# Layer two's mixers' output and MLP: the two parts of a chunk side by side in one strip of 512 columns

## The chip, the cores and the metric

The kernel runs on one core of a Trainium2 chip. The metric is the time of one execution on the device in microseconds (us). TensorE (PE) multiplies; VectorE (DVE), ScalarE (ACT) and GpSimd (POOL) do the elementwise work; SyncE (SP) issues the transfers from the chip's main memory.

## The reference

Two layers of a trunk on 16 learned meta tokens and 256 tokens, width 2048. The part around the change, cut:

```python
def _layer(h, w_in, ..., w_out, ln1_w, ln1_b, w_ff1, w_ff2, ln2_w, ln2_b):
    proj = jnp.einsum('bld,dp->blp', h, w_in)
    ...
    mix = jnp.einsum('blm,md->bld', jnp.concatenate([y_gla, y_na], axis=-1), w_out)
    h = _layer_norm(DEEPNORM_ALPHA * h + mix, ln1_w, ln1_b)
    ff = jnp.einsum('blf,fd->bld', jnp.square(jax.nn.relu(jnp.einsum('bld,df->blf', h, w_ff1))), w_ff2)
    return _layer_norm(DEEPNORM_ALPHA * h + ff, ln2_w, ln2_b)
```

The meta tokens are dropped at the end, so the second layer needs them only as keys and values: after its projection it works on T = 256 columns, where the first layer works on L = 272.

## The kernel before, in words

Activations lie transposed: a chunk is 128 features (partitions) by up to 272 tokens (columns), and 16 chunks make the width. Each is kept as two float32r parts, a high one (the rounded value) and a low one (what the rounding left), and so is each weight. A product is the sum of three: high weight by high part, high weight by low part, low weight by high part.

`three` (L156 to 167) issues them for one chunk and one tile of 128 weight columns. With 272 columns it is three matmuls, L165, L166, L167. With exactly 256 (`n == T`) the first two are one matmul of 512 columns over `x.joined` (L161), and the third (L162) adds the low weights' share onto the second half of the bank; what evicts the bank adds the halves. So in layer two each chunk and weight tile cost a **pair**, L161 and L162.

`by_m` runs over output tiles, and for each over all chunks with `three`, 16 pairs for a tile of the output (32 in the MLP's second product, which takes y and u). `by_k` (L191) runs over chunks first, with four output tiles open; it multiplies high and low part separately, also where there are 256 columns. It is used where chunks become ready one by one: the first 512 outputs of the mixers' output product, and the third group of the MLP's first product. The first two groups of that product run on chunks that aren't normalised yet and carry two columns more (`n + 2`, 258 in layer two), so they take the three matmuls.

`made` (L141 to 154) loads a weight tile of 128 x 1024 (512 KB), rounds it into `wh` on ScalarE (L152) and subtracts on VectorE for `wl` (L153); `weights` keeps two tiles ahead, the pools hold three. `order` yields the tiles in the order of use: 12 groups of the projection, 4 of the mixers' output, then the MLP. Nothing but this order and the code's own order sets what comes when around the change: a queue of generators (`fg`, `bg`) is stepped between the matmul groups, and SP issues the weights' transfers only.

Places: a chunk's two parts lie in one tile of 640 columns (`ROOM`), the first from column `home` on and the second `apart` columns later (`WIDE[layer]`); weights start at `STARTS[layer]` in a tile of 1088 columns. The tiles of x, y, u, wh and wl all begin at 64 modulo 256 bytes, so a start of 3 columns is byte 76 modulo 256. In layer two the parts are 288 columns apart, so that `x.joined` is two runs of 256 columns with a gap of 32 between them.

The chunks are x (the residual stream; written by `ln_add`, and again, normalised, by `renew`), y (the mixers' outputs, later half of the MLP's inner activations) and u (the other half). Layer two's x also serves its projection, where keys and values need all 272 columns.

Of the kernel before, what the change touches and what calls it, by code (L numbers as in the profile page):

```python
# [17 lines left out]
T = 256  # L18
# [18 lines left out]


ROOM = 640
WIDE = (23, 276), (3, 288)  # L40
STARTS = (40, 48), (0, 8)


class Pair(tuple):
# [7 lines left out]
class Trunk:  # L52
# [71 lines left out]
    def order(self):  # L124

        i, first = self.i, [4, 2]
        for l in range(DEPTH):
            groups = [i["win"][l, g] for g in range(12)] + [i["wout"][l, g] for g in range(4)]
            for half in range(2):
                groups += [i["wff1"][l, 8 * half + g] for g in range(8)] + [i["wff2"][l, half, g] for g in range(4)]  # L130
            for w in groups:
                for t in range(w.shape[0]):
                    yield w[t], first.pop(0) if first else 1, l

    def weights(self):

# [4 lines left out]
    def made(self, ap, parts, l):  # L141
        if ap is None:
            return None
        nc = self.nc
        size = ap.shape[-1]
        raw = self.wp.tile([P, WB], F32, name="raw", tag="raw")[:, :size]
        wh, wl = (self.wp.tile([P, WB + 64], F32R, name=nm, tag=nm)[:, at:at + size]
                  for nm, at in zip(("wh", "wl"), STARTS[l]))
        for p in range(parts):
            c = slice(p * size // parts, (p + 1) * size // parts)  # L150
            nc.sync.dma_start(raw[:, c], ap[:, c])
            nc.scalar.copy(wh[:, c], raw[:, c])  # L152
            self.wl = nc.vector.tensor_tensor(wl[:, c], raw[:, c], wh[:, c].bitcast(F32), ALU.subtract).ins  # L153
        return wh, wl
# [67 lines left out]
    def pair(self, pool, name, c, late=None):  # L222
        if name == "sp":
            return Pair(pool.tile([P, 2, L], F32R, name=f"{name}{c}", tag=f"{name}{c}", bufs=1))
        t = pool.tile([P, ROOM], F32R, name=f"{name}{c}", tag=f"{name}{c}", bufs=1)
        return self.parts(t, *WIDE[1 if (self.l if late is None else late) else 0])

    def parts(self, t, home, apart):

        both = t[:, home:home + 2 * apart].rearrange("p (a c) -> p a c", a=2)  # L230
        made = Pair(both)
        made.joined = both[:, :, :T]
        return made


# [214 lines left out]
    def gla_head(self, h):  # L450
# [48 lines left out]
        for at, lv in enumerate(order):  # L499
            q, k = ahead  # L500
            ahead = operands(order[at + 1]) if at + 1 < len(order) else across()
            ps = self.bank()
            for b in (slice(0, P), slice(P, T)):
                r = b if lv < 8 else slice(P - b.start, T - b.start)
                nc.tensor.matmul(ps[:, b], lhsT=k[:, b], rhs=q[:, r], start=True, stop=True)  # L505
            if full and lv <= 4:
                nc.tensor.matmul(ps[:, T:L], lhsT=k[:, T:T + P], rhs=q[:, T:L], start=True, stop=True)
            p2 = ps[:, :T].rearrange("p (s c) -> p s c", s=2)
            if lv >= 7:
                nc.scalar.copy(A[:, 0:5:4, :] if lv == 7 else A[:, 1:4:2, :], p2)  # L510
            else:
                nc.vector.copy_predicated(A[:, 0:5:4, :], self.mask[:, lv:lv + 1, :].to_broadcast([P, 2, P]), p2)
            if full and lv == 0:
                nc.vector.tensor_copy(Am[:, T:L], ps[:NM, T:L])
            elif full and lv <= 4:
                nc.vector.copy_predicated(Am[:, T:L], self.mask[:NM, lv, :NM], ps[:NM, T:L])
            yield
# [353 lines left out]
    def renew(self, end):  # L871

        f = self.norm
        n = f["n"]
        for c in range(f["new"], end):
            while f["ready"] <= c:
                self.step(self.bg, 1)
            h, lo = self.x[c]
            self.split(self.acc[:, c, :n], h[:, :n], lo[:, :n])
        f["new"] = end  # L880
# [138 lines left out]
```

## Time and profile before

| | us |
|---|---|
| median of 3 runs | 2386.49 |
| lowest, highest | 2386.22, 2386.54 |
| the profiled execution | 2386.44 |
| its span, first to last instruction | 2384.2 |

The stages of layer two, by the profile's timeline: projection and mixers from about 1237 to 1557 us, the mixers' output from 1557 to 1651, the MLP's first two groups on unnormalised chunks to 1698, the group by chunks to 1721, then the rest of the MLP to 2366, and the last normalisation.

How to read the rows: a group of instructions has its line, engine, operation, output and inputs by the program's names, the shape and the count, then busy time in us, mean duration in ns, and the idle time of the engine ahead of them with what ended it. A window has its ends, its length, each engine's busy time with the count of instructions that touch it, the granted clock, the share of the DMA engines and GB/s. A timeline row has a start, a duration (us), engine, line, operation and shape. A matmul's end is modelled, so that rows overlap: the pace is read from starts.

### The profile page before, as it was taken

What the parts mean: (1) busy time and instruction counts of PE and PEld (TensorE: products, weight loads), DVE (VectorE), ACT (ScalarE), POOL (GpSimd) and SP (SyncE); (2) the same over time, 40 slices, a digit from 0 to 9 for tenths busy, and PEclk for the clock granted to TensorE, in tenths of its full rate; (3) what the DMA queues carried; (4) which work ended last, traced back from release to release, by engine and by line L of the source; (5) the groups of instructions that cost most, each with busy time, mean ns of one, the idle gap of its engine ahead of it and who ended that gap; (6) DMA issues with size and microseconds to landing.
All of it is one profiled execution on the core that took longest, in us unless ns stands there. A gap on an engine that the chain in (4) does not pass through costs nothing.

```text
span 2384.2 us, 43078 instructions
## 1 busy us (share of the span) xinstructions
PE 2351.7 (99%) x17276; PEld 2230.9 (94%) x17276; DVE 1576.1 (66%) x2473; ACT 1187.5 (50%) x1962; POOL 283.5 (12%) x447
## 2 busy tenths in 40 slices
PE   9999999999999999999999999999999999999997
PEld 9999999999999999999999899999988888888886
DVE  6688787775544455557577887878766555666655
ACT  6555555564433344444456655555644333444443
POOL 1164320010000000000020554200100000000000
PEclk9999999999999999999999999999999999999998
DMA  7544445555555556555555445456656665656563
GB/s 248 168 142 146 143 140 160 178 179 183 178 182 180 178 181 182 178 181 179 180 177 183 142 148 153 149 160 189 192 189 191 189 190 189 190 190 191 189 188 131
DMA packets 118359, 417.46 MB, mean 175 GB/s; under 512 B 13388, under 2 KB 16332, under 8 KB 118160
## 3 DMA queue, kind: packets, MB, share of 16 engines
q1 hardware_dynamic: 118160, 414.72, 55.7%
q8 instruction: 135, 2.21, 0.4%
q14 instruction: 64, 0.52, 0.1%
HBM read 412.57 MB, written 2.10 MB: 174 GB/s over the span
## 4 chain that ended last, share of the span: by engine, by line
PE 92%; DVE 4%; POOL 2%; issue 1%; ACT 1%; DMA 0%; SPq 0%; ACTq 0%; POOLq 0%; DVEq 0%
PE mm L161 22%; PE mm L165 16%; PE mm L166 16%; PE mm L167 16%; PE mm L162 11%; PE mm L191 6%; POOL lev L475 1%; PE bg L505 1%; DVE wl L153 1%; PE bg L648 1%; DVE acc L864 1%; PE bg L597 1%; ACT wh L152 0%; ACT ns L580 0%; DVE lev L481 0%
## 5 line engine op out<-in xcount | busy, mean ns | idle before, releaser
L153 DVE TENSOR_TENSOR wl<-raw,wh 128x1024 fp32r<-128x1024 f32 (+1 forms) x772 | 945.9, 1226 | 628.7 <-ACT wh L152 620.4
L152 ACT CAST wh<-raw 128x1024 fp32r<-128x1024 f32 (+1 forms) x772 | 803.4, 1041 | 916.4 <-PE mm L166 334.0
L165 PE MATMUL mm<-x,wh 128*128 128x272 f32 (+2 forms) x2176 | 624.2, 287 | 0.0
L166 PE MATMUL mm<-x,wh 128*128 128x272 f32 (+2 forms) x2176 | 617.9, 284 | 0.0
L167 PE MATMUL mm<-x,wl 128*128 128x272 f32 (+2 forms) x2176 | 617.2, 284 | 0.1
L166 PEld LDWEIGHTS mm<-x,wh 128*128 128x128 f32 x2176 | 409.3, 188 | 0.0
L165 PEld LDWEIGHTS mm<-x,wh 128*128 128x128 f32 x2176 | 407.8, 187 | 1.2 <-issue 0.4
L167 PEld LDWEIGHTS mm<-x,wl 128*128 128x128 f32 x2176 | 407.8, 187 | 0.5 <-DVE wl L153 0.3
L161 PE MATMUL mm<-x,wh 128*128 128x512 f32 x1152 | 403.5, 393 | 0.0
L162 PE MATMUL mm<-x,wl 128*128 128x256 f32 x1152 | 320.2, 278 | 0.2 <-DVE wl L153 0.2
L161 PEld LDWEIGHTS mm<-x,wh 128*128 128x128 f32 x1152 | 215.7, 187 | 48.5 <-issue 0.4
L161 PE MATMUL mm<-y,wh 128*128 128x512 f32 x704 | 245.7, 391 | 0.0
L162 PEld LDWEIGHTS mm<-x,wl 128*128 128x128 f32 x1152 | 215.6, 187 | 0.7 <-DVE wl L153 0.6
L166 PE MATMUL mm<-y,wh 128*128 128x272 f32 x704 | 199.2, 283 | 0.0
L165 PE MATMUL mm<-y,wh 128*128 128x272 f32 x704 | 199.2, 283 | 0.0
L167 PE MATMUL mm<-y,wl 128*128 128x272 f32 x704 | 198.9, 283 | 0.0
L162 PE MATMUL mm<-y,wl 128*128 128x256 f32 x704 | 195.4, 278 | 0.6 <-DVE wl L153 0.6
L161 PE MATMUL mm<-u,wh 128*128 128x512 f32 x512 | 178.9, 391 | 0.0
L475 POOL TENSOR_TENSOR lev<-be 128x128 f32<-128x128 f32 (+1 forms) x256 | 150.2, 616 | 115.4 <-PE bg L505 36.4
L161 PEld LDWEIGHTS mm<-y,wh 128*128 128x128 f32 x704 | 132.1, 188 | 29.1
L165 PE MATMUL mm<-u,wh 128*128 128x272 f32 x512 | 144.9, 283 | 0.0
L166 PE MATMUL mm<-u,wh 128*128 128x272 f32 x512 | 144.9, 283 | 0.0
(235 smaller groups left out, 3314.0 us busy)
## 6 DMA issues: line engine op xcount, KB each, us to landing
raw<-in_wff SPq DMA_DIRECT2D x512, 512.0 KB, 3.5
raw<-in_win SPq DMA_DIRECT2D x190, 512.0 KB, 3.5
raw<-in_wout SPq DMA_DIRECT2D x64, 512.0 KB, 3.5
nb<-in_nab SPq DMA_DIRECT2D x16, 352.0 KB, 4.3
out<-acc SPq DMA_DIRECT2D x8, 256.0 KB, 2.2
xraw<-in_xT SPq DMA_DIRECT2D x7, 272.0 KB, 5.1
wraw<-in_wup SPq DMA_DIRECT2D x2, 392.0 KB
raw<-in_win SPq DMA_DIRECT2D x4, 128.0 KB, 3.1
```

The costliest lines, as they stand in the source:

```text
L152: nc.scalar.copy(wh[:, c], raw[:, c])
L153: self.wl = nc.vector.tensor_tensor(wl[:, c], raw[:, c], wh[:, c].bitcast(F32), ALU.subtract).ins
L161: mm(ps, lhsT=wh[:, c:c + P], rhs=x.joined, start=first, stop=False)
L162: mm(ps[:, T:], lhsT=wl[:, c:c + P], rhs=xh[:, :T], start=False, stop=last)
L165: mm(o, lhsT=wh[:, c:c + P], rhs=xh[:, :n], start=first, stop=False)
L166: mm(o, lhsT=wh[:, c:c + P], rhs=xl[:, :n], start=False, stop=False)
L167: mm(o, lhsT=wl[:, c:c + P], rhs=xh[:, :n], start=False, stop=last)
L191: self.nc.tensor.matmul(ps[m][:, :n], lhsT=parts[p][0][:, c:c + P], rhs=acts[j][parts[p][1]][:, :n], start=j + p == 0, stop=j == nk - 1 an ...
L475: tt = lambda o, x, y: nc.gpsimd.tensor_tensor(o, x, y, ALU.subtract)
L505: nc.tensor.matmul(ps[:, b], lhsT=k[:, b], rhs=q[:, r], start=True, stop=True)
L597: nc.tensor.matmul(ps[hh][:, t * NKEY:t * NKEY + NKEY], lhsT=q[hs, NM + t * P:NM + t * P + P], rhs=k[hs, t, :], start=True, stop=True)
L648: nc.tensor.matmul(r[hs], lhsT=(v2 if rest else v1)[:, t, hs], rhs=p2[:, t, :] if rest else p1[:, 2 * t + hh, :], start=rest, stop=not rest)
```

## The change

Layer two's y and u get a third place, (20, 256): the first part at column 20, the second right behind it at 276. `joined` is then one run of 512 columns. Layer two's x keeps its place through the projection and the first two groups of the MLP, and gets the new one when `renew` writes the normalised chunk, if there are 256 columns. The weights of layer two's mixers' output and MLP (`j > 11` of the groups) start at 36 and 4 columns in place of 0 and 8.

```diff
-WIDE = (23, 276), (3, 288)
-STARTS = (40, 48), (0, 8)
+WIDE = (23, 276), (3, 288), (20, T)
+STARTS = (40, 48), (0, 8), (36, 4)
...
-            for w in groups:
+            for j, w in enumerate(groups):
                 for t in range(w.shape[0]):
-                    yield w[t], first.pop(0) if first else 1, l
+                    yield w[t], first.pop(0) if first else 1, l + (l and j > 11)
...
-        return self.parts(t, *WIDE[1 if (self.l if late is None else late) else 0])
+        return self.parts(t, *WIDE[(2 if name != "x" else 1) if (self.l if late is None else late) else 0])
...
-        made.joined = both[:, :, :T]
+        made.tile, made.joined = t, t[:, home:home + 2 * T] if apart == T else both[:, :, :T]
...
             while f["ready"] <= c:
                 self.step(self.bg, 1)
+            if n == T:
+                self.x[c] = self.parts(self.x[c].tile, *WIDE[2])
             h, lo = self.x[c]
```

What the matmuls on float32r read in the two programs, in layer two (bytes modulo 256 of the start of the moving columns and of the weights; counts are of matmuls):

| matmuls | chunks before | weights before | chunks after | weights after |
|---|---|---|---|---|
| projection, x: 320 of 512 columns, 320 of 256, triples of 272 and 274, by chunks of 272 | 76, 204 | 64, 96 | the same | the same |
| pairs on x, y, u: 2048 of 512 columns | 76 and, 1152 bytes on, 204 | 64 | 144, one run | 208 |
| the same: 2048 of 256 columns | 76 | 96 | 144 | 80 |
| by chunks, x and y: 384 of 256 columns | 76, 204 | 64, 96 | 144, 144 | 208, 80 |
| 128 triples of 258 columns, x | 76, 204 | 64, 96 | 76, 204 | 208, 80 |

Layer one reads its chunks at 156 and 236 and its weights at 224 and 0 in both. On every engine the instructions stand in the same order, with the same waits, in both programs; only addresses and the shape of that one access differ.

## The prediction

> **What bounds the kernel now.** I read the page first: the busy shares, the row of the granted clock and the chain that ended last.
>
> ```profile
> span 2384.2 us, 43078 instructions
> PE 2351.7 (99%) x17276; PEld 2230.9 (94%) x17276; DVE 1576.1 (66%) x2473; ACT 1187.5 (50%) x1962; POOL 283.5 (12%) x447
> PEclk9999999999999999999999999999999999999998
> PE 92%; DVE 4%; POOL 2%; issue 1%; ACT 1%; DMA 0%; SPq 0%; ACTq 0%; POOLq 0%; DVEq 0%
> PE mm L161 22%; PE mm L165 16%; PE mm L166 16%; PE mm L167 16%; PE mm L162 11%; PE mm L191 6%; POOL lev L475 1%; PE bg L505 1%; DVE wl L153 1%; PE bg L648 1%; DVE acc L864 1%; PE bg L597 1%; ACT wh L152 0%; ACT ns L580 0%; DVE lev L481 0%
> ```
>
> TensorE sets the end: busy 99%, its clock at full all along, its lines 92% of the chain. But a busy matmul row says little about how fast matmuls follow each other, since their ends are modelled and overlap. What counts here is the distance from start to start. So I next took the groups of lines 161 and 162 from 1557 us (where layer two's mixers' output begins) to the end, and then windows and timelines inside stretches in which only one kind of matmul runs.
>
> ```profile
> L161 PE MATMUL mm<-x,wh 128*128 128x512 f32 x832 | 288.5, 391 | 0.0
> L161 PE MATMUL mm<-y,wh 128*128 128x512 f32 x704 | 245.7, 391 | 0.0
> L162 PE MATMUL mm<-x,wl 128*128 128x256 f32 x832 | 231.0, 278 | 0.0
> L162 PE MATMUL mm<-y,wl 128*128 128x256 f32 x704 | 195.4, 278 | 0.6 <-DVE wl L153 0.6
> L161 PE MATMUL mm<-u,wh 128*128 128x512 f32 x512 | 178.9, 391 | 0.0
> L162 PE MATMUL mm<-u,wl 128*128 128x256 f32 x512 | 142.4, 278 | 0.0
> ```
>
> These are all the matmuls that get the strip: 832 + 704 + 512 = 2048 pairs of one 512-column matmul (both parts of a chunk) and one of 256 (the high part again, with the low weights). TensorE sat idle ahead of them for 0.6 us in all. Now their pace, first the pair in layer two's MLP, then the three matmuls of 272 columns that layer one uses for the same product. Each stretch is shown by the count of one line in it and the first and last start of that line.
>
> ```profile
> 2010.00:2185.00 175.00, 175.00 (x506) 1.00 0.61 190
> 2010.34 0.39 PE L161 MATMUL mm<-x,wh 128*128 128x512 f32 x1
> 2010.57 0.28 PE L162 MATMUL mm<-x,wl 128*128 128x256 f32 x1
> 2010.68 0.39 PE L161 MATMUL mm<-x,wh 128*128 128x512 f32 x1
> ...
> 2184.71 0.39 PE L161 MATMUL mm<-x,wh 128*128 128x512 f32 x1
> 815.00:1025.00 210.00, 162.14 (x573) 1.00 0.59 179
> 815.35 0.28 PE L165 MATMUL mm<-y,wh 128*128 128x272 f32 x1
> ...
> 1024.71 0.28 PE L165 MATMUL mm<-y,wh 128*128 128x272 f32 x1
> ```
>
> Of the 506 rows of line 161 two began before the window, so 504 starts lie between 2010.34 and 2184.71: 174.37 / 503 = **346.7 ns a pair**. Of the 573 of line 165 one began before: 209.36 / 571 = **366.7 ns a triple**. A pair moves 768 columns, a triple 816. The difference, 20.0 ns for 48 columns, is 0.417 ns a column. Taking that as the price of a column (estimate from these two rows), 768 columns cost 320.0 ns and 816 cost 340.0, and **both leave 26.7 ns over**. Both read three stretches of memory: the triple high, low, high; the pair high and low in one instruction, 1152 bytes apart, then high. So 26.7 ns is 8.9 ns for each stretch. The rows inside a pair point the same way: the 512-column one with its two stretches takes 0.23 us to the next start, some 16.7 ns over 213.3, and the 256-column one (2010.57 to 2010.68, 0.11 to 0.12 us) 10 over 106.7.
>
> **Does the place in memory matter?** The same instructions at other addresses, or with other lengths, in this trace:
>
> ```profile
> 1290.58 0.28 PE L166 MATMUL mm<-x,wh 128*128 128x272 f32 x1
> ...
> 1292.80 0.28 PE L166 MATMUL mm<-x,wh 128*128 128x272 f32 x1
> 1659.90:1697.00 37.10, 29.07 (x102) 1.00 0.55 173
> 1699.00:1720.00 21.00, 21.00 (x183) 1.00 0.61 185
> ```
>
> - Layer two's projection has the triple of 272 columns with the parts at 76 and 204 and the weights at 64 and 96 modulo 256; between the first two rows lie six of them: 2.22 / 6 = 370.0 ns, against 366.7 in layer one (156 and 236, 224 and 0). So place is worth at least 3.3 ns a triple; leftover 10.0 a stretch.
> - The triple of 258 columns, line 165 again: 101 starts from 1659.9 on, 37.0 / 101 = 366 to 367 ns, as long as with 272 columns. Its columns cost 322.5, so 44.2 over, 14.7 a stretch: the dearest.
> - The k-outer stage (line 191, one stretch of 256 columns each): 183 less the 2.4 that were running at the start, 21.00 / 180.6 = 116.3 ns, 9.6 over.
>
> The steady paces, 346.7, 366.7 and 370.0, are all multiples of 3.33 ns (104, 110 and 111 of them). I take it that a pace settles on that grid.
>
> **The change, part by part.**
>
> 1. The strip: 2048 pairs go from three stretches to two. At 8.9 ns a stretch a pair becomes 320.0 + 17.8 = 337.8 ns, at 9.6 339.2, at 10.0 340.0. I take **340.0**, the first point of the grid that covers all three: 6.67 ns a pair, 2048 x 6.67 = **13.65 us**. The bounds: two stretches at 14.7 give 349.4, a loss of 2.7 ns x 2048 = 5.6 us. On the other side no row for this type of data shows less than 8.9. The nearest cheaper row is that of plain f32 matmuls:
>
> ```profile
> 1400.66 0.59 PE L538 MATMUL bg<-A,V 128*128 128x256 f32 x2
> 1401.09 0.59 PE L539 MATMUL bg<-A,V 128*128 128x256 f32 x2
> ```
>
> Two such matmuls of 256 columns take 0.43 us, 215 ns each: about the 213.3 of 512 columns by the price above, so I read them as two steps a column (estimate), and 1.7 ns over. Two stretches at 1.7 would give 323.4, a gain of 23.3 ns x 2048 = 48 us. These matmuls draw their columns at half the pace, so I hold that end far off; between it and 8.9 the value is nearer 8.9.
>
> 2. New places, for those pairs: the parts at 144, the weights at 208 and 80, instead of 76, 204, 64 and 96. Priced above only as the spread (8.9 to 14.7 a stretch); the layer-one and projection triples show 1.1 ns a stretch for a change of place alone. Value taken: nothing, for want of a row at these places.
>
> The TensorE page of the Trainium skill (TensorE: Matmul & The Clock Gate, section "Wait — 56ns, not 53.3ns?") has warm matmuls start N / 2.4 GHz plus about 2.5 ns apart, with no term for place or for runs of memory. By it the pair would be 325 ns, before and after, and the sum zero; the trace has 346.7 and does not agree, while its f32 rows nearly do.
>
> 3. The 128 triples of 258 columns keep their chunks and get the moved weights; the 384 k-outer matmuls (192 on y, 192 on x) get both new places. Value nothing. Bounds: a triple at 360 to 373.3 ns, -0.9 to +0.8 us; the k-outer ones at 8.9 to 14.7 over, 115.6 to 121.4 ns, -0.3 to +2.0 us.
>
> 4. ScalarE's and VectorE's writes land elsewhere (weights, y, u, x). Cost nothing: they are hidden behind the matmuls.
>
> ```profile
> L153 DVE TENSOR_TENSOR wl<-raw,wh 128x1024 fp32r<-128x1024 f32 x286 | 350.2, 1225 | 258.5 <-ACT wh L152 255.0
> 2030.00:2160.00 130.00, 130.00 (x752) 113.88 (x751) 82.99 (x117) 62.51 (x94) 0.00 (x0) 1.00 0.61 190
> 1600.00:1640.00 40.00, 40.00 (x233) 34.93 (x232) 37.08 (x76) 20.08 (x28) 0.00 (x0) 1.00 0.70 209
> ```
>
> (The last two rows are TensorE, its weight loads, VectorE, ScalarE and GpSimd, then clock and DMA.) Eight pairs use up one weight tile in 2.77 us; VectorE spends 1.23 us on it. In the MLP VectorE is busy 64%, DMA 0.61. At 340.0 ns a tile is due every 2.72 us, 2% sooner: room enough. The one thin cover is the mixers' output: VectorE is busy 37.08 of 40 us there, and the wait of 0.6 us above stands there too. Its 192 pairs would gain 1.3 us, and that is the most that VectorE can take back. Nothing is moved in any queue and no wait is added.
>
> **Sum.** The profiled execution took 2386.44 us (span 2384.2), 0.05 below the median of 2386.49. 2386.49 - 13.65 = **2372.8 us**.
>
> **The rivals.**
>
> - *The leftover belongs to the weights, not to the stretches.* Pair and triple both use one high and one low weight tile, and 26.7 ns for each such set fits them as well. Then the strip changes nothing: 346.7 ns, 2386.5 us. Against it: the split of the leftover inside the pair, 16.7 and 10. The rule of the Trainium skill named above comes to the same end, no change. Chance 0.13.
> - *The new places are better than any in the trace.* Two stretches at 6.7 ns, 333.3 a pair: 13.3 x 2048 = 27.3 us, 2359.2. For it: a strip that ends where the next begins, modulo 256, and 44.2 against 26.7 for a mere 258 columns, so much hangs on phases. Chance 0.14; lower paces still, 0.06.
> - *Slower: the strip's stretches cost what those of 258 columns do.* Place: every pair. Price: 14.7 ns each, on the grid 350.0 ns, +3.33 x 2048 = +6.8 us, 2393.3. It decides from 13.3 ns a stretch on (26.7 / 2), the point where two cost what three did. The 258-column rows show that weights and chunks can fall into such a phase for a whole stage. Chance 0.08, and 0.09 for 353.3 or more (2400 us and up).
>
> **How the numbers follow.** The forecast, paces from 336.7 to 343.3 ns (2366 to 2380 us): 0.50. Range: from the good places with the low bounds of part 3 (2359.2 - 1.2) to the 350-ns rival: 2358 to 2394, which holds 0.50 + 0.14 + 0.13 + 0.08 = 0.85; without any one end it would fall under 0.8. A measurement of this kernel tells some 0.2%, 4.8 us, from no change. Faster: 0.50 + 0.14 + 0.06 = 0.70; same 0.13; slower 0.17.
>
> **What would show it.** Starts of line 161 in the MLP 340.0 ns apart would show the stretches right; 346.7 the weights' rival. If the gain sits in the 256-column matmul and not in the 512-column one (0.23 us to the next start), the place did it and not the strip. Line 162's waits for the low weights in the mixers' output should stay under 2 us. I am wrong altogether if the pace differs between x, y and u, since all have the same places.

## The result and the profile after

| | before | after |
|---|---|---|
| median, us | 2386.40 (2386.22 to 2386.54, 4 runs) | 2372.11 (2371.65 to 2372.29, 4 runs) |
| ratio, 95% interval | | 0.9940 [0.9923, 0.9957] |
| profiled execution, span | 2386.44, 2384.2 | 2372.29, 2370.1 |

A second series gave 2371.98 against 2386.07, ratio 0.994 [0.9926, 0.9955]. The change makes the kernel 14.3 us (0.6%) faster; 2372.8 was forecast.

From the page of the kernel after: span, busy shares, granted clock and the chain by engine.

```profile
span 2370.1 us, 43078 instructions
PE 2337.7 (99%) x17276; PEld 2223.8 (94%) x17276; DVE 1576.1 (66%) x2473; ACT 1188.2 (50%) x1962; POOL 283.5 (12%) x447
PEclk9999999999999999999999999999999999999998
PE 91%; DVE 4%; POOL 2%; issue 1%; ACT 1%; DMA 0%; SPq 0%; ACTq 0%; POOLq 0%; DVEq 0%
```

TensorE's busy time fell by 14.0 us and the span by 14.1; the other engines and the clock stayed. Next, for the kernel before and then for the one after, the window 2020 to 2170 us in layer two's MLP, counting line 161 alone (window, length, busy time and count, clock, DMA share, GB/s).

```profile
2020.00:2170.00 150.00, 150.00 (x434) 1.00 0.61 190
```

```profile
2020.00:2170.00 150.00, 150.00 (x442) 1.00 0.58 194
```

One row in each was running when the window opened, so 433 and 441 pairs begin in 150 us: 346.4 and 340.1 ns. (The count is whole, so this reading is good to 0.8 ns.) The timeline after shows the same from the starts:

```profile
2099.69 0.39 PE L161 MATMUL mm<-x,wh 128*128 128x512 f32 x1
2099.91 0.28 PE L162 MATMUL mm<-x,wl 128*128 128x256 f32 x1
2100.03 0.39 PE L161 MATMUL mm<-x,wh 128*128 128x512 f32 x1
...
2101.05 0.39 PE L161 MATMUL mm<-x,wh 128*128 128x512 f32 x1
```

Four pairs from 2099.69 to 2101.05: 1.36 / 4 = 340 ns. By stages, each from the first start of its kind of matmul to that of the next kind, in the two traces (us; the MLP's pairs to the start of the last one, and the last row to the end of the span):

| stage | before | after | less |
|---|---|---|---|
| up to the mixers' output | 1558.12 | 1557.85 | 0.26 |
| its first 512 outputs, by chunks | 25.16 | 25.08 | 0.08 |
| its 192 pairs | 67.93 | 67.09 | 0.84 |
| 128 triples of 258 columns | 47.30 | 46.55 | 0.75 |
| third group of the MLP, by chunks | 22.37 | 22.29 | 0.08 |
| 1856 pairs of the MLP | 644.30 | 632.19 | 12.11 |
| after the last pair's start | 19.06 | 19.04 | 0.02 |

So far this looks as forecast, step for step. The experiments say otherwise about why.

### The profile page after: what moved, and what is told of

Its sections match the earlier page's. It is cut to its first block, busy times and chain, and to the rows that moved or that the text cites. A ratio compares the mean times of both kernels' runs of the same rounds, so it can differ in the third digit from the quotient of the medians.

```text
span 2370.1 us, 43078 instructions
## 1 busy us (share of the span) xinstructions
PE 2337.7 (99%) x17276; PEld 2223.8 (94%) x17276; DVE 1576.1 (66%) x2473; ACT 1188.2 (50%) x1962; POOL 283.5 (12%) x447
## 4 chain that ended last, share of the span: by engine, by line
PE 91%; DVE 4%; POOL 2%; issue 1%; ACT 1%; DMA 0%; SPq 0%; ACTq 0%; POOLq 0%; DVEq 0%
PE mm L161 21%; PE mm L165 16%; PE mm L166 16%; PE mm L167 16%; PE mm L162 11%; PE mm L191 6%; POOL lev L475 1%; PE bg L505 1%; DVE wl L153 1%; PE bg L648 1%; DVE acc L864 1%; PE bg L597 1%; DVE lev L481 0%; ACT wh L152 0%; ACT ns L580 0%
## 5 line engine op out<-in xcount | busy, mean ns | idle before, releaser
L161 PE MATMUL mm<-x,wh 128*128 128x512 f32 x1152 | 398.0, 391 | 0.0
```

What stands on the lines that cost most here:

```text
L161: mm(ps, lhsT=wh[:, c:c + P], rhs=x.joined, start=first, stop=False)
```

## The experiments

Three theories. **A**, the prediction's: each stretch of memory that a matmul reads costs some 9 ns, and the strip saves one of three. **B**: the places of chunk and weights modulo 256 bytes set the pace, and the strip is worth nothing. **C**: the weights' place alone does it. A time given without a range is that of one run, beside the kernel before in the same series.

### The new places with a gap (e1_gap)

```diff
-WIDE = (23, 276), (3, 288), (20, T)
+WIDE = (23, 276), (3, 288), (20, 320)
...
-        both = t[:, home:home + 2 * apart].rearrange("p (a c) -> p a c", a=2)
+        if apart == 320:
+            both = t.rearrange("p (a c) -> p a c", a=2)[:, :, home:]
+        else:
+            both = t[:, home:home + 2 * apart].rearrange("p (a c) -> p a c", a=2)
```

> The parts keep their new places modulo 256 bytes (both at 144) and the weights theirs (208, 80), but the low part lies 320 columns after the high one, so the 512-column matmul reads two stretches with a gap of 64 columns. Theory A (each stretch of memory costs some 9 ns, the gain comes from one stretch less): the pair goes back to 346.7 ns, some 2386 us. Theory B (the places modulo 256 decide, a gap costs nothing): 340.0 ns a pair, 2372 us. In between would mean that both count.

Measured: 2372.04 us, beside 2385.92 of the kernel before. The same window, line 161:

```profile
2020.00:2170.00 150.00, 150.00 (x442) 1.00 0.62 194
```

442 again, 340 ns: the full gain with two stretches in the 512-column matmul and 64 columns between them. Theory A falls: the second stretch costs nothing here.

### The strip at the old places (e2_strip_old_places)

```diff
-WIDE = (23, 276), (3, 288), (20, T)
-STARTS = (40, 48), (0, 8), (36, 4)
+WIDE = (23, 276), (3, 288), (3, T)
+STARTS = (40, 48), (0, 8), (0, 8)
```

> One strip of 512 columns, but from byte 76 modulo 256 on, and all weights of layer two at 64 and 96 as before the change. Theory A (stretches): 340.0 ns a pair, 2372 to 2373 us. Theory B (places): 346.7 ns or another pace that isn't 340.0; at 346.7 some 2386 us.

Measured: 2386.88 us.

```profile
2020.00:2170.00 150.00, 150.00 (x434) 1.00 0.62 190
```

434, as before the change: the strip without the new places is worth nothing. (In a strip the low part can't keep its old place: it moves from 204 to 76. One could think that this move took the strip's gain back; e1, where a gap costs nothing, and lines 64 and 65 of bench1 below speak against it.)

### The weights alone (e3_weights_only)

```diff
-WIDE = (23, 276), (3, 288), (20, T)
+WIDE = (23, 276), (3, 288), (3, 288)
```

> Only the weights of the mixers' output and the MLP move (208, 80); the chunks stay as before, 288 columns apart from byte 76 on. Theory A: 346.7 ns a pair; only the 128 triples of 258 columns get faster (366.7 to 360 ns, 0.9 us), 2385.5 us. Theory C (the weights' place alone decides): 340.0 ns a pair, 2372 us.

Measured: 2392.03 us, 6.1 more than the kernel before.

```profile
2020.00:2170.00 150.00, 150.00 (x429) 1.00 0.60 188
```

428 starts, 350 ns a pair: theory C falls too, and the places belong together. The triples of 258 columns, whose chunks did not move, did get faster. Their line 165, in the window in which the kernel before has 102 rows and 366.7 ns:

```profile
1659.90:1697.00 37.10, 28.84 (x103) 1.00 0.55 177
```

103 rows, by their starts 360.0 ns apart.

### TensorE alone (bench1)

Each stretch is one line like this one (stretch of line 65; `x` and `w` take a place in bytes modulo 256, a count of columns and, for two runs, their distance in columns):

```python
for k in range(48): mm(ps[k % 4], lhsT=w(k, 208), rhs=x(k, 144, 256, 320), **f); mm(ps[k % 4][:, 256:], lhsT=w(k, 80, 1), rhs=x(k, 144, 256), **f)
```

> TensorE alone: weights and chunks are loaded once, then 72 stretches of 48 pairs (or triples, or single matmuls) follow each other, each on a source line of its own; the rest of the computation is left out. The stretch with the places of before must show 346.7 ns a pair and that of the change 340.0, or the pace depends on the other engines. Theory A: strips cost 340 at whatever place, two runs 346 or more; single matmuls of 512 and 256 columns at one place cost the same over 0.417 ns a column, 7 to 10 ns. Theory B: the pace changes with the place of chunk or weights and not with the gap, and single matmuls cost some 4 to 8% over 0.417 ns a column, in proportion to their length. With 32 columns of weights in place of 128 the pace falls if weight reads collide with chunk reads, and stays if the chunk reads alone set it.

Its timeline has one row for a line; from the start of a row to that of the next is what its 48 pairs took.

```profile
41.25 16.80 PE L63 MATMUL ps<-x,w 128*128 128x512 f32 x96
57.90 16.50 PE L64 MATMUL ps<-x,w 128*128 128x512 f32 x96
74.23 16.48 PE L65 MATMUL ps<-x,w 128*128 128x512 f32 x96
90.55 17.11 PE L66 MATMUL ps<-x,w 128*128 128x512 f32 x96
107.50 16.80 PE L67 MATMUL ps<-x,w 128*128 128x512 f32 x96
124.14 16.80 PE L68 MATMUL ps<-x,w 128*128 128x512 f32 x96
140.78 16.81 PE L69 MATMUL ps<-x,w 128*128 128x512 f32 x96
157.43 16.96 PE L70 MATMUL ps<-x,w 128*128 128x512 f32 x96
174.23 17.11 PE L71 MATMUL ps<-x,w 128*128 128x256 f32 x144
191.18 17.13 PE L72 MATMUL ps<-x,w 128*128 128x256 f32 x144
```

| line | chunk | weights | ns a pair |
|---|---|---|---|
| 63 (before) | 76, low part 288 columns on | 64, 96 | 16.65 / 48 = 347 |
| 64 (after) | strip at 144 | 208, 80 | 16.33 / 48 = 340 |
| 65 | 144, low part 320 columns on (144) | 208, 80 | 16.32 / 48 = 340 |
| 66 | 144, low part 288 columns on (16) | 208, 80 | 16.95 / 48 = 353 |
| 67 | strip at 76 | 64, 96 | 16.64 / 48 = 347 |
| 68 | strip at 76 | 208, 80 | 16.64 / 48 = 347 |
| 69 | strip at 144 | 64, 96 | 16.65 / 48 = 347 |
| 70 | 76, low part 288 columns on | 208, 80 | 16.80 / 48 = 350 |

The other engines are idle meanwhile. The window 40 to 1000 us (TensorE, its weight loads, VectorE, ScalarE, GpSimd, clock, DMA share, GB/s):

```profile
40.00:1000.00 960.00, 960.00 (x5707) 846.14 (x5706) 0.00 (x0) 0.00 (x0) 0.00 (x0) 1.00 0.00 1
```

The paces are still those of the whole kernels, so the other engines and the transfers have no part in them. Lines 64, 67, 68 and 69 are the same strip with chunk and weights at the old or the new place: both must be new. Lines 65 and 66 differ in the distance of the low part alone, 13 ns. With the weights at 208 and 80, sixteen strips from byte 0 to 240 in steps of 16 gave 340.0 ns at 16 and 144 only, and 344 to 353 at the other fourteen. Line 71 has the same work at the new places in three matmuls of 256 columns, the two parts in different tiles: 16.95 / 48 = 353 ns. So the place is good for this pair, not for every cut of the columns.

### Shifts, exchanges, and single matmuls (bench2)

> TensorE alone again, 201 stretches; the rest of the computation is left out. Theory B1 (only the distance between a chunk's start and the weights' start counts, modulo 128 bytes): all sixteen shifts of chunk and weights together by multiples of 16 bytes give 340.0 ns a pair; 208/80, 80/208, 208/208 and 80/80 all give 340.0, with the chunk at 144 and at 16. Theory B2 (absolute places, or the order of the two weights' places, count): some of these give 346.7 or more. Moving only the weights by 4 to 28 bytes: under both a part of these steps give 346.7 to 353.3; under B1 the best lies alone. A single 512-column matmul over and over: if reads of chunk and weights collide, its pace changes with the weights' place; if the chunk alone sets it, all eight places give one pace. Matmuls of 64 and 128 columns: the time of a weight load alone, some 111 ns, and less with 32 columns of weights if a load's length counts.

Rows of its timeline, each line 36 pairs or 36 single matmuls: strip and weights of the change shifted together by 16 bytes (line 67), 32 (68) and 48 (69); strip at 144 with weights at 80/208 (83), 208/208 (84) and 80/80 (85); and one 512-column matmul over and over at 144, with weights at 0 (121), 160 (126) and 192 (127).

```profile
91.74 12.85 PE L67 MATMUL ps<-x,w 128*128 128x512 f32 x72
104.42 12.44 PE L68 MATMUL ps<-x,w 128*128 128x512 f32 x72
116.69 12.86 PE L69 MATMUL ps<-x,w 128*128 128x512 f32 x72
129.39 12.43 PE L70 MATMUL ps<-x,w 128*128 128x512 f32 x72
...
291.46 12.44 PE L83 MATMUL ps<-x,w 128*128 128x512 f32 x72
303.73 12.88 PE L84 MATMUL ps<-x,w 128*128 128x512 f32 x72
316.45 12.64 PE L85 MATMUL ps<-x,w 128*128 128x512 f32 x72
328.93 12.46 PE L86 MATMUL ps<-x,w 128*128 128x512 f32 x72
...
634.74 8.55 PE L121 MATMUL ps<-x,w 128*128 128x512 f32 x36
643.13 8.47 PE L122 MATMUL ps<-x,w 128*128 128x512 f32 x36
...
676.47 8.33 PE L126 MATMUL ps<-x,w 128*128 128x512 f32 x36
684.64 8.61 PE L127 MATMUL ps<-x,w 128*128 128x512 f32 x36
693.08 8.56 PE L128 MATMUL ps<-x,w 128*128 128x512 f32 x36
```

- Shift by 16: 12.68 / 36 = 352 ns over the whole stretch, 353.3 once steady; by 32: 12.27 / 36 = 341, steady 340.0; by 48: 12.70 / 36 = 353. All sixteen go that way: the eight multiples of 32 at 340.0, the odd multiples of 16 at 353.3.
- Exchanged weights (12.27 / 36) hold the 340; both weights at 208 (12.72 / 36) or both at 80 (12.48 / 36) do not. So it isn't the distance to the chunk modulo 128 alone (B1), since 208 and 80 are equal by that; at this place of the chunk, and at 16 too, only weights 128 bytes apart gave 340.
- Moving only the weights by 4 to 28 bytes either way gave 346.7 to 353.3 once steady: the 340 stands alone.
- The 512-column matmul with its chunk at one place takes 233, 227 and 234 ns as only the weights' place changes. So the reading of the weights bears on the pace of the matmul that runs. How is not shown: bench1 was to see a faster matmul with 32 weights in place of 128 if the two reads collide, and at 144 and 208 it saw none (229.0 ns both).

### All of layer two, and the weights exchanged (e4, e5)

```diff
 # e4, on top of e1
-WIDE = (23, 276), (3, 288), (20, 320)
-STARTS = (40, 48), (0, 8), (36, 4)
+WIDE = (23, 276), (20, 320), (20, 320)
+STARTS = (40, 48), (36, 4), (36, 4)
 # e5, on top of the change
-STARTS = (40, 48), (0, 8), (36, 4)
+STARTS = (40, 48), (0, 8), (4, 36)
```

> The layout of e1_gap (parts 320 columns apart, both at 144) for all of layer two, its projection included, and all of layer two's weights at 208 and 80. Theory B (places): the projection's 320 pairs go from 346.7 to 340.0 ns too, 2.1 us less than the change, 2370 us, give or take what its 448 triples of 272 and 274 columns do at places not yet seen (366.7 to 380 ns: -1.5 to +4.5 us). Theory A has no gain for them.

Measured: 2374.42 us. The projection's pairs did go to 340 ns, but its triples of 272 columns from 370 to some 378 (near the worst end of what was expected), which costs more.

> The change with the high weights at 80 and the low ones at 208. Theory B1 (the distance modulo 128 bytes): 340.0 ns a pair, 2372 us as with the change. Theory B2 (each weight's place modulo 256): another pace, 346.7 ns or more, 2386 us or more.

Measured: 2372.55 us, 442 rows in the window: 340 ns, as bench2 has it. That is what B1 said, and not what B2 said as it was put there; what speaks against B1 is bench2's 208/208 stretch and its shift by 16 bytes.

### Everything 16 bytes further on (e7)

```diff
-WIDE = (23, 276), (3, 288), (20, T)
-STARTS = (40, 48), (0, 8), (36, 4)
+WIDE = (23, 276), (3, 288), (24, T)
+STARTS = (40, 48), (0, 8), (40, 8)
```

> The change with everything 16 bytes further on: strip from 160, weights at 224 and 96; distances and contiguity as in the change. Theory A and B1 (distances): 340.0 ns a pair, 2372 us. Theory B2 (absolute places on a grid of 32 bytes, as in bench2): 353.3 ns a pair, 13.3 ns x 2048 = 27 us more than the change, some 2399 us, slower than before.

Measured: 2397.30 us beside 2386.07 of the kernel before.

```profile
2020.00:2170.00 150.00, 150.00 (x426) 1.00 0.58 186
```

425 starts, 353 ns. The same strip, the same distances, four columns further: 25 us slower than the change and 11 slower than the kernel before.

### A version meant to beat the change (e6)

```diff
 # on top of e4
-STARTS = (40, 48), (36, 4), (36, 4)
+STARTS = (40, 48), (36, 36), (36, 4)
...
-                    yield w[t], first.pop(0) if first else 1, l + (l and j > 11)
+                    pairs = j > 11 or j in (2, 4, 5) or j > 5 and (4 * (j - 6) + t // 2) % 3 == 0
+                    yield w[t], first.pop(0) if first else 1, l + (l and pairs)
```

> The layout of e1_gap for all of layer two, and in the projection the weights' place by the kind of product: 208 and 80 for the groups that run as pairs, 208 and 208 for those that run as triples of 272 or 274 columns (369.9 ns there in bench2, against 370.0 in the kernel before). By theory B2 (places): the projection's 320 pairs at 340.0 ns, 2.1 us less than the change, its triples as before; the 128 triples of 258 columns at some 355 ns as in e4, 0.6 us less. 2369.5 us, ratio to the kernel before 0.993. Theory A has none of this: 2372 us.

> The change once more, beside e6 on the same chip: 2372.1 us, ratio 0.994, by every theory.

Measured side by side: e6 2373.55 us (2373.05 to 2373.65), ratio 0.9946 [0.993, 0.9963]; the change 2371.98 (2371.84 to 2372.23). A miss: the two ranges don't touch. The timeline of e6 in its projection (line 166 is the first matmul of a triple there):

```profile
1294.95 0.29 PE L166 MATMUL mm<-x,wh 128*128 128x272 f32 x1
...
1296.47 0.29 PE L166 MATMUL mm<-x,wh 128*128 128x272 f32 x1
```

Four triples in 1.52 us, 380 ns each, where bench2 had 370.0 with the same places modulo 256 (line 151). The pairs gained as expected, the triples lost more. The low part's tile differs between the two (the same tile in the kernel, another in bench2); whether that is it wasn't tried.

## Why the prediction came out right

The time was right by luck: the step that gave it was wrong.

- **What bounds the kernel**: right. TensorE's pace carried the whole gain, and the sum 2048 x 6.67 = 13.65 us compares with 12.11 + 0.84 = 12.95 in the two stages of pairs. The missing 0.7 lies in the mixers' output, where 0.44 of the 1.28 did not come, and in the MLP (0.26). The thin cover of the mixers' output did take something back, but less than that: line 162's one wait for low weights there grew from 0.6 to 0.7 us. The rest lies in pairs at or just behind a break in the sequence, which take longer than the steady pace in both kernels, and a little more so in the one after (in the MLP nine such pairs make 0.21 of the 0.26).
- **The step that failed**: "The strip: 2048 pairs go from three stretches to two", 8.9 to 10 ns each. e1 has three stretches and the whole gain, e2 two and none of it. That the pair of before and the triple of layer one both left 26.7 ns over was taken as a price per stretch. But that equality was no evidence: the price of a column, 0.417 ns, was the difference of these two paces over 48 columns, and with it the two leftovers must come out equal. In the runs the leftover goes with the place and not with the count of stretches: the bench's strips, two stretches each, leave 20.0 to 46.7 by the same price.
- **"New places ... Value taken: nothing, for want of a row"**: this was the whole of it. The spread of 1.1 ns a stretch, read from the two triples, was far too small: strips that differ in place alone run from 340.0 to 366.7 ns (chunk at 132, weights at 208 and 80), 55 us over 2048 pairs.
- **The test laid down beforehand pointed there**: the prediction said that a gain in the 256-column matmul speaks for the place. Over the 512 pairs on u, the mean distance from the start of line 161 to that of 162 fell from 229.4 to 226.6 ns, and from 162 to the next 161 from 117.2 to 113.5: more than half of it in the matmul whose one stretch stayed one. By the prediction's step all 6.67 ns would lie in the other. At 340.0 the leftover is about 13.3 on 512 columns and 6.7 on 256, in proportion to the columns. The x, y and u stretches all run at 340.0, as said.
- **The rival "the new places are better than any in the trace"** was the right mechanism, with its size over-estimated (333.3). The rival by which the leftover belongs to the weights had one half right: the strip by itself changes nothing (e2). But the leftover isn't fixed for a set of weights, since it moves with their place and the chunk's. The slower rival is real as a case, but by place: 350 in e3 and 353.3 in e7, where it was put down to stretches.
- **The grid**: right for the pairs of e1 to e7, which run at 340.0, 346.7, 350.0 or 353.3 ns, and not in general. Some stretches of bench1 hold a pace between its points: strips at byte 0 (weights at 208 and 80) 344.5 ns, at 128 351.1. Taking the first grid point above 337.8 to 340.0 is what made a wrong step land on the right number.
- **Weights moved under the 258-column triples**: nothing was forecast, with bounds from a gain of 0.9 us to a loss of 0.8. They gained 0.75 in the execution shown above. In the profiled execution of the second series, of the same kernel, they took 45.80 us, a gain of 1.50, which is outside the bounds (last section). By chunks: a gain of 0.16, within the bounds.

The same page of the Trainium skill, TensorE: Matmul & The Clock Gate, says in "Step-by-step: what each phase is for" that the next weights' load takes no SBUF bandwidth from the running matmul, since the two have read ports of their own. For float32r the running matmul is not left alone by the weights all the same: moving only the weights took a 512-column matmul from 227 to 234 ns (bench2, lines 126 and 127). Whether that is read bandwidth, no run here shows.

What stays open is the rule by which a place is good. Every layout of the pair that ran at 340.0 had the chunk's start 16 bytes past a multiple of 32 and the two weights 128 bytes apart, each 64 bytes from the chunk modulo 128; what meets what inside TensorE was not shown. Nor do the places modulo 256 settle everything: the triples of e6 run 10 ns apart in kernel and bench at equal places, and those of 258 columns have two paces in one kernel.

## What to carry to other kernels

When dense float32r matmuls set the time, the start of the moving columns and of the weights modulo 256 bytes is a parameter worth some 4% of them here (340.0 to 353.3 ns a pair), and a bench of TensorE alone can find it: it reproduced the whole kernels' paces for pairs, though not for the triples of e6. A change that moves data and also reshapes it should be split in two before it is explained: here the reshaping was worth nothing. A layout that is best for one shape of matmul may be bad for another on the same tile (e6: 340 for pairs, 380 for triples).

## What the runs showed of the hardware

- Two single matmuls that differ by 16 columns can differ by 13 ns: at 144 and 208, 256 columns start 113.3 ns apart, 272 columns 126.6 (bench1, steady).
- 256 columns at that place are near a floor. Rows of bench1, 256 and 192 columns wide, 48 matmuls each, every one with weights of its own:

```profile
267.44 5.62 PE L79 MATMUL ps<-x,w 128*128 128x256 f32 x48
272.90 5.50 PE L80 MATMUL ps<-x,w 128*128 128x192 f32 x48
278.23 11.17 PE L81 MATMUL ps<-x,w 128*128 128x512 f32 x48
```

  5.46 / 48 = 114 ns and 5.33 / 48 = 111 ns: a quarter of the columns less saves almost nothing. Rows of bench2, 36 matmuls each, of 128 and 64 columns with 128 weights, then the same with 32 weights:

```profile
701.48 4.13 PE L129 MATMUL ps<-x,w 128*128 128x128 f32 x36
705.45 4.77 PE L130 MATMUL ps<-x,w 128*128 128x64 f32 x36
710.03 4.03 PE L131 MATMUL ps<-x,w 128*32 128x128 f32 x36
713.86 2.03 PE L132 MATMUL ps<-x,w 128*32 128x64 f32 x36
715.72 13.46 PE L133 MATMUL ps<-x,w 128*128 128x272 f32 x108
```

  With 128 weights 110 and 127 ns, with 32 weights 106 and 52: at 64 columns the number of weights sets the pace.
- At 512 columns (229.0 ns) and at 256 (113.3), with the chunk at 144 and the weights at 208, loading 32 weights in place of 128 changed nothing. The weights' place does change both: 226.7 to 234.6 and 113.3 to 120.0 ns (bench2, chunk at 144, steady).
- One sequence at fixed places can hold two steady paces. The triple of 258 columns in the kernel before ran at 360 ns for its first tile (16 triples) and at 366.7 from then on. Two executions of the kernel after differ the same way; line 165 from 1660 to 1695 us, in the first series and in the second:

```profile
1660.00:1695.00 35.00, 27.24 (x98) 1.00 0.55 181
1660.00:1695.00 35.00, 27.54 (x100) 1.00 0.58 182
```

  By the starts 360.0 and 353.3 ns, the same program at the same places. The stage was 0.75 us shorter in the second. What picks the pace is not shown.
